# Queue places for the weight sums of an MLP's second map: behind the neighbouring product's split and weight load

## The chip, the cores and the metric

The kernel runs on one core of one Trainium2 chip. Its time is the device time of one execution in microseconds (us); the time of a kernel is the median of three runs. Five engines with a queue each take part: PE (TensorE, matmuls), DVE (VectorE, additions and subtractions), ACT (ScalarE, copies and activations), POOL (GpSimd, here only for issuing DMAs that store) and SP (SyncE, only for issuing DMAs, nearly all loads). An engine takes the instructions of its queue in order, so one that waits holds up all behind it; only PE's weight loads run beside its matmuls.

## The reference

One layer of a decoder, S = 2048 tokens, D = 1024, hidden width 4096, fp32:

```python
h = x * (1.0 + sc1) + sh1
z = h @ w_in[l]                                   # token mixing: conv and pooling groups
...
x = _layer_norm(DEEPNORM_ALPHA * x + (1.0 + g1) * mix, ln1_g[l], ln1_b[l])
h = x * (1.0 + sc2) + sh2
f = jnp.square(jax.nn.relu(h @ w_mlp_in[l])) @ w_mlp_out[l]
x = _layer_norm(DEEPNORM_ALPHA * x + (1.0 + g2) * f, ln2_g[l], ln2_b[l])
```

## The kernel before

**Stages.** The tokens are worked on in two halves of 1024 (b = 0 and 1). For each half come the input projection, the output projection with the first norm, and then the **first map** (`first_map(b)`: h times w_mlp_in, ReLU, square). After both halves, one **second map** (`down`) multiplies the squared hidden values of all 2048 tokens by w_mlp_out and ends with the last norm. The text calls the first maps of the two halves map 0 (about 280 to 700 us of the profiled span) and map 1 (about 920 to 1265 us).

**Products.** Every fp32 operand is split in two: `hi`, a copy rounded by ACT (L135), and `lo`, the rest, subtracted by DVE (L136). Three matmuls (L140, L141, L142: hi·hi, hi·lo, lo·hi) stand for one fp32 matmul; the L142 one is the only one that reads the weight's `lo`. Maps are computed by Strassen's method in Winograd's form: seven products of sums of blocks instead of eight products of blocks. In the first map a block of 512 hidden columns (`up(b, g, …)`, g = 0 to 7) takes seven products of 24 matmuls each. For each product `product` (inside `seven`) takes a raw weight tile `r` of 128x1024 (a block of w_mlp_in, or a sum of blocks), splits it into a pair of `w` tiles, and runs the matmuls into two PSUM banks. Tiles of a name share a ring of fixed size: r 5, w 6 (three pairs), o 10, h 28, PSUM 8.

**Where the weights of the first map come from.** In map 0, from g = 2 on, `block_weights` loads four raw blocks (SP, L566), forms the sums on DVE and stores them for map 1 (`w1sum`); in map 1, and for g < 2, `summed_weights` loads each tile as it is (SP, L598).

**Work beside the products in the first map.** Results in PSUM are added by DVE (`add`, `o<-o,ps` rows at L145), made ReLU and square by ACT, and then `sums` forms the quarter sums that the second map's Strassen form wants (DVE, 128x256 rows at L145), each stored by POOL to `usum` (L1058).

**The weight sums of the second map** (`sum_down`, L1124 to L1137). The second map has 26 products, and most of them want a sum of blocks of w_mlp_out (`in_w2`). They are formed in eight groups. A group takes three `o` tiles (L1126) and holds them over its 11 **steps**; in all it has 12 loads of 128x512 (SP, L1136, 256 KB each), 20 additions of 128x512 (DVE, L145) and 17 stores to `wsum` (POOL, L1134, 256 KB each). The first step only loads; each later one adds, stores and reloads half tiles, so that a reload waits for the store of what stood there, and a later addition waits for the reload.

A step is traced where `next` is called on the generator. In map 0, `first_side` first yields a few other pieces, with 16 steps among them, then all the steps that are left, one per call; in map 1 the side is the generator itself; `down` takes one step per position of its stream. In the maps the call is `beside()`, 48 times in each map after the opening products (1 in g = 0, 5 in g = 1, 7 in each later block). The second map's stream has a position for each pair of a product and a quarter of the contraction (`gp`), 24 matmuls each; its operands are four positions ahead: a load of `r<-usum`, a load of `w<-in_w2` or `w<-wsum` (L1173, L1175), a split each into `h` tiles.

**What sets the order.** The order in which code is traced is not the order of an engine's queue. A scheduler places every instruction in its engine's queue by its own reckoning of when its inputs are there, and may set work that is traced later ahead of work that waits. `with tc.issue_after(x)` holds it back in one respect: instructions traced in the block that run on x's engine stand behind x in that engine's queue. It is an order of the queue, not a wait of its own.

Of the kernel before, what the change touches and what calls it, by code (L numbers as in the profile page):

```python
# [97 lines left out]
def tile_hybrid_layer(ctx: ExitStack, tc: tile.TileContext, opening, xT, x, wada, win,  # L98
# [23 lines left out]
    def t_w(dt=F32R):  # L122
        return mk(big, [P, T], dt, "w", 6)
# [10 lines left out]
    def split(src, hi, lo):  # L134
        high = nc.scalar.copy(hi, src)  # L135
        return high.ins, nc.vector.tensor_tensor(lo, src, hi.bitcast(F32), op=ALU.subtract).ins  # L136
# [7 lines left out]
    def tt(out_, a, b_, op):  # L144
        return nc.vector.tensor_tensor(out_, a, b_, op=op)  # L145
# [183 lines left out]
    def parts(src, t=t_h):  # L329
        hi, lo = t(), t()  # L330
        split(src, hi, lo)
        return hi, lo
# [224 lines left out]

    RAW = range(4)  # L560
    ORDER = (("11", "11"), ("12", "21"), ("s2", "2"), ("s1", "1"), ("s3", "3"), ("s4", "22"), ("22", "4"))

    def block_weights(src, dst=None):
        a11, a12, a21, a22 = [t_r() for _ in range(4)]
        for i, r in enumerate((a11, a12, a21, a22)):
            nc.sync.dma_start(r, src[i])  # L566
        yield a11
        yield a12
        s1 = t_r()
        tt(s1, a21, a22, ALU.add)  # L570
        tt(a21, a11, a21, ALU.subtract)
        tt(a11, s1, a11, ALU.subtract)
        tt(a12, a12, a11, ALU.subtract)
        if dst is not None:
            for i, r in enumerate((s1, a11, a21, a12)):
                nc.gpsimd.dma_start(dst[i], r)
        for r in (a11, s1, a21, a12, a22):
            yield r
# [16 lines left out]
    def summed_weights(src, sums, order):  # L595
        for i in order:
            r = t_r()
            nc.sync.dma_start(r, src[i] if i in RAW else sums[i - 4])  # L598
            yield r

    def seven(ready, B, first_w=None):
        made = [first_w] if first_w else []

        def product(i, banks, new):
            hi, lo = made.pop() if made else parts(next(ready), t_w)
            for p in range(2):
                if new:
                    banks[p] = t_ps()
                for k in range(4):
                    bh, bl = B[ORDER[i][1], k // 2]  # L610
                    ks = slice((k % 2) * H, (k % 2) * H + H)
                    cs = slice(p * H + k * P, p * H + k * P + P)
                    mm3(banks[p], hi[:, cs], lo[:, cs], bh[:, ks], bl[:, ks], new and k == 0, k == 3,
                        not new)

        return product
# [406 lines left out]
    def up(b, g, B, beside, turn):  # L1023
# [11 lines left out]

        def add(r, banks):
            for p in range(2):
                tt(r[:, ps[p]], r[:, ps[p]], banks[p], ALU.add)

        def join(r, banks):  # L1040
            add(r, banks)
# [112 lines left out]
    def down(g2, close, side):  # L1154
# [92 lines left out]
        for k, (n, gp) in enumerate(stream):  # L1247
            if n == last:
                break
            next(side, None)  # L1250
            if k + 4 < len(stream):
                ready.append(operand(*stream[k + 4]))
            ops = ready.pop(0)
            _, _, _, new, reads = PRODUCTS[n]
            if gp == 0:
                if new:
                    banks[n % 2] = [t_ps() for _ in range(4)]
                if 3 <= n < 12:
                    next(later)
            for i in range(4):  # L1260
                unit(banks[n % 2][i], i, ops, new and gp == 0, gp == 3, not new)
            if gp == 3:
                for t, d, c in reads:
                    read(t, d, c, banks[n % 2])
                    if final[t, d] == n:
                        finish(t, d)
# [82 lines left out]
    def first_side():  # L1349
        for n in range(0, 8, 2):  # L1350
            ada(G2 + n, G2 + n + 2, nc.sync.dma_start, lambda: t_o(D))
            yield
        for n in range(4):
            for _ in range(4):
                next(sums_down)
                yield
            sum_x(n)
            yield
        g2 = mk(sm, [P, D], F32, "bc", 1)
        row_by_dram(g2, mod[:, G2 : G2 + KD], 1)  # L1360
        gate.append(g2)
        for p in halves:
            sum_weights(wins[0], winsum, t_o, which=[p])
            yield
        for _ in sums_down:
            yield

    gate = []
# [2 lines left out]
    def first_map(b, B, back):  # L1371
        side = sums_down if b else first_side()
        open_ = []

        def beside():
            if open_:
                next(side, None)

        def turn():
            if b + 1 < NB:  # L1380
                ready.append(prepare())

        ups = [up(b, g, B, beside, turn) for g in range(NC)]
        for g in range(2):
            next(ups[g])
            back(1 + g)
        for i in range(3, 7):
            next(ups[0])
            back(i)
        open_.append(True)  # L1390
        for g in range(NC):
            for _ in ups[g]:
                pass
# [62 lines left out]
```

## Time and profile before

| | |
|---|---|
| runs | 1849.01, 1844.09, 1844.26 us; median 1844.26 us |
| profiled execution | 1848.79 us, of which the span of the profile is 1846.8 us |
| PE busy | 1726.5 us (93% of the span), 7519 matmuls |
| DVE busy | 1420.4 us (77%) |
| ACT, POOL busy | 840.1 us (45%), 402.7 us (22%) |
| moved by DMA | 478.95 MB, mean 259 GB/s |
| stores to wsum | 136 of 256 KB, median 4.5 us from issue to landing |
| loads of blocks for the sums (o<-in_w) | 104 of 256 KB, median 5.0 us (8 of them for the input projection's sums) |

All times in the rows below are us from the start of the span. In a row of a group of instructions (`line engine op out<-in`), the last columns are the busy time, the mean duration of one, and the time that the engine stood idle just before them with what ended it. In a row of stretches, `(x178)` is the number of instructions, and the last three columns are the clock that TensorE was granted, the busy share of the DMA engines and the GB/s. A row of waits reads: which line waited for which line, us in total, how many times, longest. In a row of the timeline the first column is the start, the second the time that the merged instructions took together; consecutive instructions start a little before the one ahead has ended, so that two 128x512 additions in a row start 0.60 us apart though each takes 0.69 us.

### The profile page before, as it was taken

The page shows a single profiled execution, that of the slowest core. Times are in us where ns is not written, and L with a number is a line of the kernel's source. Part 1 is how long each engine was busy: PE and PEld are TensorE (multiplying, and loading weights), DVE is VectorE, ACT ScalarE, POOL GpSimd, SP SyncE. Part 2 cuts the span into 40 slices and gives each one's busy share as a digit, 9 for nine tenths or more (in the row PEclk, how much of TensorE's full clock was granted, in tenths as well). Part 3 has the DMA queues.
Part 4 walks back from the last instruction along what each step waited for, and adds up shares of the span by engine and source line. Part 5 has one row for each costly group of instructions (what it writes and reads, how often), then busy time and mean ns, then how long its engine had stood idle before and what let it go on. Part 6 is the DMA issues. An engine that isn't in the chain of part 4 may idle for free. (4 is left out here: it accounts for less than half of the span.)

```text
span 1846.8 us, 22581 instructions
## 1 busy us (share of the span) xinstructions
PE 1726.5 (93%) x7519; PEld 1415.0 (77%) x7519; DVE 1420.4 (77%) x2222; ACT 840.1 (45%) x1148; POOL 402.7 (22%) x767
## 2 busy tenths in 40 slices
PE   9999998777959889999988999899999999999998
PEld 8888886656747768888866777677888888888887
DVE  7997886687877877689676677777666586686998
ACT  6322475334534465344754344453644334353552
POOL 0223121244454531010113454443000000000000
PEclk9999998888989999999989999999999999999999
DMA  9998864588988896257545798898967787676772
GB/s 389 349 337 316 305 248 158 184 300 296 314 291 289 287 309 232 100 189 260 185 158 173 268 292 288 276 304 307 353 235 260 247 281 282 219 249 219 266 279 80
DMA packets 155205, 478.95 MB, mean 259 GB/s; under 512 B 22600, under 2 KB 23120, under 8 KB 155088
## 3 DMA queue, kind: packets, MB, share of 16 engines
q1 hardware_dynamic: 100960, 304.44, 47.8%
q0 software_dynamic: 54128, 173.07, 26.1%
q8 instruction: 59, 0.97, 0.2%
q14 instruction: 58, 0.48, 0.1%
HBM read 315.40 MB, written 162.01 MB: 259 GB/s over the span
## 5 line engine op out<-in xcount | busy, mean ns | idle before, releaser
L140 PE MATMUL ps<-h,w 128*128 128x512 f32 x1312 | 523.9, 400 | 58.8 <-ACT w L135 34.5
L142 PE MATMUL ps<-h,w 128*128 128x512 f32 x1312 | 522.7, 399 | 38.2 <-DVE w L136 38.2
L141 PE MATMUL ps<-h,w 128*128 128x512 f32 x1312 | 521.9, 398 | 8.1 <-DVE h L136 8.0
L141 PE MATMUL ps<-h,h 128*128 128x512 f32 (+1 forms) x1064 | 414.3, 389 | 3.5 <-DVE h L136 3.5
L140 PE MATMUL ps<-h,h 128*128 128x512 f32 (+1 forms) x1064 | 414.0, 389 | 0.8 <-ACT h L135 0.8
L142 PE MATMUL ps<-h,h 128*128 128x512 f32 (+1 forms) x1064 | 414.1, 389 | 0.0
L140 PEld LDWEIGHTS ps<-h,w 128*128 128x128 f32 x1312 | 252.5, 193 | 118.5 <-ACT w L135 37.3
L142 PEld LDWEIGHTS ps<-h,w 128*128 128x128 f32 x1312 | 253.1, 193 | 97.6 <-DVE w L136 44.6
L145 DVE TENSOR_TENSOR o<-o,o 128x256 f32<-128x256 f32 (+2 forms) x554 | 266.0, 524 | 70.5 <-DMA o<-in_w 23.9
L141 PEld LDWEIGHTS ps<-h,w 128*128 128x128 f32 x1312 | 253.1, 193 | 64.3 <-DVE h L136 11.1
L1058 POOL DMA_DIRECT2D usum<-o x416 | 222.9, 541 | 245.6 <-DVE o L145 172.9
L135 ACT CAST w<-r 128x1024 fp32r<-128x1024 f32 x156 | 163.4, 1050 | 203.5 <-PE ps L141 175.9
L135 ACT CAST h<-r 128x1024 fp32r<-128x1024 f32 (+1 forms) x144 | 144.8, 1011 | 240.4 <-PE ps L141 131.1
L141 PEld LDWEIGHTS ps<-h,h 128*128 128x128 f32 x1064 | 200.6, 189 | 45.3 <-DVE h L136 4.3
L136 DVE TENSOR_TENSOR h<-r,h 128x1024 fp32r<-128x1024 f32 (+1 forms) x144 | 167.5, 1170 | 86.0 <-ACT h L135 85.8
L140 PEld LDWEIGHTS ps<-h,h 128*128 128x128 f32 x1064 | 200.7, 189 | 42.5 <-ACT h L135 1.6
L142 PEld LDWEIGHTS ps<-h,h 128*128 128x128 f32 x1064 | 200.6, 189 | 40.8
L136 DVE TENSOR_TENSOR w<-r,w 128x1024 fp32r<-128x1024 f32 x156 | 190.0, 1222 | 49.4 <-ACT w L135 48.7
L145 DVE TENSOR_TENSOR o<-o 128x256 f32<-128x256 f32 (+1 forms) x240 | 124.9, 528 | 69.2 <-DMA o<-in_w 38.6
L145 DVE TENSOR_TENSOR o<-o,ps 128x512 f32<-128x512 f32 x172 | 114.1, 683 | 22.9 <-PE ps L142 19.5
L136 DVE TENSOR_TENSOR h<-w,h 128x1024 fp32r<-128x1024 f32 x104 | 126.8, 1220 | 1.6 <-ACT h L135 1.5
L1134 POOL DMA_DIRECT2D wsum<-o x136 | 73.5, 541 | 191.3 <-DVE o L145 185.1
(163 smaller groups left out, 1382.4 us busy)
## 6 DMA issues: line engine op xcount, KB each, us to landing
usum<-o POOLq DMA_DIRECT2D x416, 128.0 KB, 4.9
r<-usum SPq DMA_DIRECT2D x104, 512.0 KB, 5.1
wsum<-o POOLq DMA_DIRECT2D x136, 256.0 KB, 4.5
w<-wsum SPq DMA_DIRECT2D x68, 512.0 KB, 5.6
r<-in_w SPq DMA_DIRECT2D x54, 512.0 KB, 5.3
o<-in_w SPq DMA_DIRECT2D x104, 256.0 KB, 5.0
r<-w1sum SPq DMA_DIRECT2D x40, 512.0 KB, 4.8
w<-in_w SPq DMA_DIRECT2D x36, 512.0 KB, 6.3
```

The lines of the kernel that those rows point to most:

```text
L135: high = nc.scalar.copy(hi, src)
L136: return high.ins, nc.vector.tensor_tensor(lo, src, hi.bitcast(F32), op=ALU.subtract).ins
L140: nc.tensor.matmul(ps, whi, xhi, start=first, stop=False, skip_group_check=goes_on)
L141: nc.tensor.matmul(ps, whi, xlo, start=False, stop=False, skip_group_check=goes_on)
L142: nc.tensor.matmul(ps, wlo, xhi, start=False, stop=last, skip_group_check=goes_on)
L145: return nc.vector.tensor_tensor(out_, a, b_, op=op)
L1058: nc.gpsimd.dma_start(usum[slot, g // 2, :, b, g % 2, :], z)
L1134: nc.gpsimd.dma_start(wsum[i - 8, g // 2][:, cs], regs[to])
```

## The change

Four things change.

1. Two **marks** are kept while the program is traced: the last load of a first-map weight on SP, and the last `lo` half of a weight split or the last half of a PSUM addition on DVE, whichever was traced later.
2. In both maps `beside()` traces its step inside two `issue_after` blocks, one for each mark: the step's DVE work stands behind the DVE mark, its SP loads behind the SP mark. ACT and POOL get no mark.
3. `first_side` ends with 17 steps (3 · 11 − 16) instead of all that are left, so that map 0 forms exactly three groups (33 steps); its last 5 calls find nothing. Before, map 0 traced 38 steps: three groups and 5 steps of the fourth.
4. `down` takes two steps per position instead of one. Map 1 takes 48 steps in both kernels; before, that leaves 2 of the 88 for `down`, now 7.

```diff
@@ block_weights, summed_weights
+    mark = {}
...
-            nc.sync.dma_start(r, src[i])
+            mark["SP"] = nc.sync.dma_start(r, src[i]).ins
...
-            nc.sync.dma_start(r, src[i] if i in RAW else sums[i - 4])
+            mark["SP"] = nc.sync.dma_start(r, src[i] if i in RAW else sums[i - 4]).ins
@@ seven
-            hi, lo = made.pop() if made else parts(next(ready), t_w)
+            if made:
+                hi, lo = made.pop()
+            else:
+                r = next(ready)
+                hi, lo = t_w(), t_w()
+                mark["DVE"] = split(r, hi, lo)[1]
@@ up
-                tt(r[:, ps[p]], r[:, ps[p]], banks[p], ALU.add)
+                mark["DVE"] = tt(r[:, ps[p]], r[:, ps[p]], banks[p], ALU.add).ins
@@ down
-            next(side, None)
+            for _ in range(2):
+                next(side, None)
@@ first_side
-        for _ in sums_down:
+        for _ in range(3 * len(W_SUMS) - 16):
+            next(sums_down)
             yield
@@ first_map
-                next(side, None)
+                with tc.issue_after(mark["DVE"]), tc.issue_after(mark["SP"]):
+                    next(side, None)
```

Every engine has as many instructions as before; only their order in the queues differs. Three places show it. Names carry a running number for the tile (`o_692`), so the same tile may have other numbers in the two programs; line numbers behind the diff's first lines grow by 1 to 9 (L1136 becomes L1142, L598 becomes L599, L664 becomes L670).

**First place: SP's queue at the end of map 0**, where the loads of the second half's input projection begin (`in_xT`, `xsum`: the tokens and their sums; `in_wins`, `winsum`: its weights). `o_692` to `o_694` are the three tiles of the fourth group of weight sums. Before:

```order
L598 DMA r_703_5176<-in_wins 128x1024
L664 DMA r_706_5182<-in_xT 128x2x512
L1136 DMA o_692_5080<-in_w2 128x512 x2
L1136 DMA o_693_5081<-in_w2 128x512
L664 DMA r_709_5191<-in_xT 128x2x512
L1136 DMA o_694_5082<-in_w2 128x512
L1136 DMA o_692_5080<-in_w2 128x512
L664 DMA r_712_5200<-in_xT 128x2x512
L664 DMA r_715_5209<-in_xT 128x2x512
L1136 DMA o_694_5082<-in_w2 128x512
```

With the change:

```order
L599 DMA r_700_5159<-in_wins 128x1024
L670 DMA r_703_5165<-in_xT 128x2x512
L670 DMA r_706_5174<-in_xT 128x2x512
L670 DMA r_709_5183<-in_xT 128x2x512
L670 DMA r_712_5192<-in_xT 128x2x512
L670 DMA r_715_5201<-xsum_147 128x2x512
L670 DMA r_718_5207<-xsum_147 128x2x512
L670 DMA r_730_5348<-xsum_147 128x2x512
```

The fourth group's loads are gone from here, and with them its additions on DVE; before, the scheduler had set all 11 steps of it ahead, those that are traced only in map 1 too. In the changed kernel they stand in map 1.

**Second place: DVE's queue in map 1** between the splits of two weight tiles that follow each other (`w_1129`, `w_1133`, block g = 1; 1005 to 1008 us of the profile before). The `o_1107` to `o_1109` rows of 128x512 with no `ps` are additions of the fourth group; the 128x256 rows are quarter sums. Before:

```order
L145 TENSOR_TENSOR o_1109_7646<-o_1109_7646,o_1032_7206 128x256
L136 TENSOR_TENSOR w_1129_7865<-r_1127_7862,w_1128_7864 128x1024
L145 TENSOR_TENSOR o_1109_7646<-o_1109_7646,o_1032_7206 128x256
L145 TENSOR_TENSOR o_1113_7701<-o_1113_7701,ps_1117_7715 128x512
L136 TENSOR_TENSOR w_1133_7920<-r_1131_7917,w_1132_7919 128x1024
```

With the change the second split has 17 instructions between it and the first (one row stands for two); the last eleven and the split:

```order
L145 TENSOR_TENSOR o_1106_7621<-o_1029_7181,o_1106_7621 128x256
L145 TENSOR_TENSOR o_1106_7621<-o_1106_7621 128x256
L145 TENSOR_TENSOR o_1080_7445<-o_1080_7445,o_1106_7621 128x256
L145 TENSOR_TENSOR o_1106_7621<-o_1106_7621 128x256
L145 TENSOR_TENSOR o_1107_7642<-o_1107_7642,o_1109_7644 128x512
L145 TENSOR_TENSOR o_1106_7621<-o_1106_7621,o_1029_7181 128x256
L145 TENSOR_TENSOR o_1108_7643<-o_1107_7642,o_1108_7643 128x512
L145 TENSOR_TENSOR o_1106_7621<-o_1106_7621,o_1029_7181 128x256
L145 TENSOR_TENSOR o_1119_7718<-o_1119_7718,ps_1051_7286 128x512
L145 TENSOR_TENSOR o_1119_7718<-o_1119_7718,ps_1052_7299 128x512
L145 TENSOR_TENSOR o_1108_7643<-o_1108_7643,o_1107_7642 128x512
L136 TENSOR_TENSOR w_1133_7897<-r_1131_7894,w_1132_7896 128x1024
```

The first split has moved ahead of the quarter sums, and steps of the fourth group stand ahead of the second.

**Third place: SP's queue at the start of the second map.** The `r<-usum` and `w<-in_w2` loads of 128x1024 are its operands; `o_1301` to `o_1303` before and `o_1327` to `o_1329` now are the eighth group's tiles. Before:

```order
L1173 DMA r_1353_9952<-usum_140 128x1024
L1136 DMA o_1303_9512<-in_w2 128x512
L1136 DMA o_1302_9511<-in_w2 128x512
L1136 DMA o_1303_9512<-in_w2 128x512
L1136 DMA o_1301_9510<-in_w2 128x512
L1175 DMA w_1342_9930<-in_w2 128x1024
L1175 DMA w_1348_9942<-in_w2 128x1024
L1136 DMA o_1302_9511<-in_w2 128x512
L1175 DMA w_1354_9954<-in_w2 128x1024
```

With the change:

```order
L1179 DMA r_1353_9930<-usum_140 128x1024
L1142 DMA o_1327_9730<-in_w2 128x512 x2
L1142 DMA o_1328_9731<-in_w2 128x512
L1181 DMA w_1342_9908<-in_w2 128x1024
L1142 DMA o_1327_9730<-in_w2 128x512
L1181 DMA w_1348_9920<-in_w2 128x1024
L1142 DMA o_1329_9732<-in_w2 128x512
L1181 DMA w_1354_9932<-in_w2 128x1024
L1181 DMA w_1360_9944<-in_w2 128x1024
L1142 DMA o_1329_9732<-in_w2 128x512
```

Before, the loads above are the last of the eighth group. Now they are its first, and six more follow further down, between the operand loads of the positions that come later (the last of them stands behind the operands of position 11). On DVE the group's additions stand accordingly between the splits of the second map's operands.

## The prediction

> **What bounds the kernel now.** I read the page's busy shares first, then PE's row in 40 slices, then the stretches of 40 us, then what PE waits for in the two first maps.
>
> ```profile
> PE 1726.5 (93%) x7519; PEld 1415.0 (77%) x7519; DVE 1420.4 (77%) x2222; ACT 840.1 (45%) x1148; POOL 402.7 (22%) x767
> PE   9999998777959889999988999899999999999998
> ```
>
> PE is the bound, and the slices below 9 lie where the first maps run (a slice is 46 us; counted from 0, slices 6 to 14 are 277 to 692 us, and 20, 21 and 25 lie between 923 and 1200). What can be won is PE's lost time there. The stretches give it:
>
> ```profile
> 400.00:440.00 40.00, 40.00 (x178) 33.13 (x178) 31.58 (x51) 21.51 (x25) 15.33 (x29) 1.00 0.90 314
> 640.00:680.00 40.00, 34.66 (x141) 27.59 (x140) 30.01 (x51) 28.62 (x37) 13.39 (x25) 0.91 0.90 301
> 680.00:720.00 40.00, 34.85 (x141) 27.66 (x140) 31.35 (x42) 21.88 (x28) 8.65 (x17) 0.91 0.92 312
> 1000.00:1040.00 40.00, 40.00 (x178) 33.12 (x178) 29.79 (x61) 20.61 (x25) 19.76 (x37) 1.00 0.76 240
> 1040.00:1080.00 40.00, 36.20 (x152) 29.13 (x151) 32.46 (x61) 16.69 (x20) 19.06 (x37) 0.96 0.87 270
> 1080.00:1120.00 40.00, 36.97 (x163) 30.31 (x162) 27.50 (x53) 18.47 (x22) 18.48 (x35) 1.00 0.85 295
> 1160.00:1200.00 40.00, 33.92 (x141) 26.93 (x140) 30.01 (x58) 13.89 (x18) 18.26 (x35) 0.96 0.84 281
> 1200.00:1240.00 40.00, 38.21 (x169) 31.34 (x168) 30.33 (x58) 18.85 (x23) 20.15 (x38) 1.00 0.92 301
> 1240.00:1280.00 40.00, 37.16 (x149) 29.47 (x148) 30.98 (x58) 17.80 (x21) 16.67 (x31) 0.91 0.87 310
> 1280.00:1320.00 40.00, 38.47 (x169) 31.35 (x168) 26.18 (x24) 27.38 (x34) 3.22 (x6) 1.00 1.01 375
> ```
>
> A stretch without loss holds 178 matmuls, 0.225 us each, so a product of 24 takes 5.4 us. One with 141 has lost 37 · 0.225 = 8.3 us, of which 5.3 us is idle and the rest is matmuls issued slowly after an idle piece, at a granted clock of 0.91. By the same sum 1040, 1080, 1160 and 1200 lost 5.8, 3.4, 8.3 and 2.0 us, together **19.5 us**; 1240 and 1280 lost 6.5 and 2.0. What PE waits for, first from 280 to 720, then from 960 to 1260:
>
> ```profile
> PE ps L140 <- ACT w L135: 34.5, 6, 18.6
> PE ps L142 <- DVE w L136: 25.5, 9, 10.0
> ```
>
> ```profile
> PE ps L142 <- DVE w L136: 12.7, 5, 3.6
> ```
>
> So in map 1 the late thing is the weight's `lo` half, a subtraction on DVE. DVE is busy only three quarters of the time: the split is late because of what stands ahead of it. In map 1 this is, by shape:
>
> ```profile
> L145 DVE TENSOR_TENSOR o<-o,o 128x256 f32<-128x256 f32 x120 | 44.1, 420 | 1.2 <-ACT o L1046 1.1
> L145 DVE TENSOR_TENSOR o<-o,o 128x512 f32<-128x512 f32 x42 | 28.9, 689 | 13.1 <-DMA o<-in_w 12.6 <-DMA usum<-o 0.3
> L145 DVE TENSOR_TENSOR o<-o 128x512 f32<-128x512 f32 x30 | 20.5, 690 | 29.8 <-DMA o<-in_w 23.5 <-DMA usum<-o 3.6 <-issue 2.7
> ```
>
> The 128x256 rows are quarter sums; the two 128x512 rows hold the weight sums, at whose head DVE stands 36 us for their loads.
>
> **The change, term by term**, against the profiled execution (1848.8 us, of which 1846.8 is span), whose stage lengths I take. The instruction counts don't change, so nothing is saved or paid but waiting. SP's loads and POOL's stores move with each step.
>
> **Term D, map 1's dense places (gain).** A group before is done in about seven products, now over nine to eleven, as the order has it. The worst place before:
>
> ```profile
> 1092.81 1.23 DVE L136 TENSOR_TENSOR w<-r,w 128x1024 fp32r<-128x1024 f32 x1
> ...
> 1107.36 0.69 DVE L145 TENSOR_TENSOR o<-o 128x512 f32<-128x512 f32 x1 [2.34 <-DMA o<-in_w]
> ...
> 1110.44 1.22 DVE L136 TENSOR_TENSOR w<-r,w 128x1024 fp32r<-128x1024 f32 x1
> ```
>
> ```profile
> 1111.72 0.50 PE L142 MATMUL ps<-h,w 128*128 128x512 f32 x1 [3.03 <-DVE w L136]
> ```
>
> Two splits lie 17.6 us apart; two products of PE take 10.8. Between them stand 23 quarter sums (0.335 us start to start, as the two rows at 621 below show), 7 weight sums and an addition from PSUM (0.60 each), and waits for loads of 3.9 us. In the changed queue the matching pair has the same 23 and 5, the PSUM additions being elsewhere, and I put the wait at 2.4: 7.7 + 3.0 + 2.4 = 13.1 us. That still exceeds 10.8, by 2.3 where it was 6.8. Splits are made ahead into three pairs, so some of that is covered, but the start of a group still falls on the longest run of quarter sums. I take half of the 19.5 us: **+9.8**, with bounds of 0 (gaps only change place) and 19.5 (all gone).
>
> **Term C, the fourth group's start now in map 1 (loss).** The stretch from 1000 had all 178 matmuls and gets the first half of the fourth group: between the splits of w_1129 and w_1133 stand 17 instructions instead of 2, about 7.5 us instead of 0.9, and reloads to wait for. The three stretches of before with a group's start (1080, 1160, 1200) lost 3.4, 8.3 and 2.0, on average **−4.6**, which I take; bounds 0 and −8.3.
>
> **Term B, the end of map 0 (gain).** There the fourth group goes away. From 640 to 700 PE waits:
>
> ```profile
> PE ps L142 <- DVE w L136: 5.9, 4, 2.1
> PE ps L140 <- ACT w L135: 4.6, 2, 2.5
> ```
>
> That is 10.5 us, of which one wait of 1.3 lies ahead of the fourth group, beside the third:
>
> ```profile
> 641.53 0.50 PE L142 MATMUL ps<-h,w 128*128 128x512 f32 x1 [1.27 <-DVE w L136]
> ```
>
> For the others SP and DVE show the cause: SP's queue, what it waits for between 655 and 700, and DVE:
>
> ```profile
> 681.98 0.35 SPq L1136 DMA_DIRECT2D o<-in_w  x1
> 682.43 0.38 SPq L598 DMA_DIRECT2D r<-winsum  x1
> ```
>
> ```profile
> SPq L1136 <- DMA wsum<-o: 10.7, 3, 6.8
> ```
>
> ```profile
> 690.06 1.22 DVE L136 TENSOR_TENSOR h<-r,h 128x1024 fp32r<-128x1024 f32 x1 [1.12 <-ACT h L135]
> ```
>
> The load of the next product's weight stands behind a reload of the fourth group that waited for a store; the splits come late from there. With the group gone, the waits of 9.2 us (10.5 less 1.3) and their slow restarts can go, about 5 of the 6.1 us (two stretches of 8.3, less 10.5 idle). The loads of the input projection's tokens and sums still have to come, 512 KB each. I take **+11** of 14.2; bounds 0 and 14.2.
>
> The skill bears on the slow restarts. The Trainium skill, in "TensorE: Matmul & The Clock Gate", Part 1, says that the array falls to half clock after an idle window of about 3.4 us, of a counter that runs free. By this, the waits here (the longest 2.5 us) would cost only themselves, and terms B and D would be about 8 and 8. The trace only half agrees: 640 to 680 has no wait over 2.5 us and was granted 0.91, while 1080 to 1120 with one of 3.03 us was granted 1.00.
>
> **Term A, the middle of map 0 (both signs).** The marks act in map 0 too. The wait for DVE that takes longest there, and another:
>
> ```profile
> 450.99 0.69 DVE L145 TENSOR_TENSOR o<-o,o 128x512 f32<-128x512 f32 x1 [4.07 <-ACT o L642]
> 451.60 1.22 DVE L136 TENSOR_TENSOR w<-r,w 128x1024 fp32r<-128x1024 f32 x1
> ```
>
> ```profile
> 621.46 0.42 DVE L145 TENSOR_TENSOR o<-o 128x256 f32<-128x256 f32 x1
> 621.79 0.42 DVE L145 TENSOR_TENSOR o<-o,o 128x256 f32<-128x256 f32 x1
> ...
> 624.40 1.22 DVE L136 TENSOR_TENSOR w<-r,w 128x1024 fp32r<-128x1024 f32 x1
> ```
>
> ```profile
> 625.68 0.64 PE L142 MATMUL ps<-h,w 128*128 128x512 f32 x1 [2.64 <-DVE w L136]
> ```
>
> At 451 the split that PE waited 10.0 us for stood right behind the addition that waited for ACT. Now six instructions stand between: a 128x1024 subtraction (1.14 us) and five of 128x512 (0.60 each), 4.1 us later. At 534 two weight sums now precede the subtraction that PE's 18.6 us wait hangs on: −1.5. At 638, four weight sums more ahead of a split: −2.4. At 624 the split now stands ahead of the seven quarter sums and two PSUM additions that held it: the wait of 2.6 us can go, with its restart, +4 (my estimate, 1.4 for the restart). Sum **−4**; bounds −9 (nothing regained at 624, restarts elsewhere) and +4.
>
> **Term E, the start of the second map.** The eighth group moves behind the map's end: 12 loads and 17 stores of 256 KB, 7.6 MB, into a stretch whose DMA engines are full (1280 to 1320: share 1.01, 375 GB/s). What carries its prices:
>
> ```profile
> SPq L1136 <- DMA wsum<-o: 93.9, 26, 7.3
> ```
>
> ```profile
> wsum<-o POOLq DMA_DIRECT2D x136, 256.0 KB, 4.5
> o<-in_w SPq DMA_DIRECT2D x104, 256.0 KB, 5.0
> ```
>
> ```profile
> 1259.14 0.86 SPq L1175 DMA_DIRECT2D w<-in_w  x2
> ```
>
> ```profile
> 1268.23 0.80 PE L141 MATMUL ps<-h,h 128*128 128x512 f32 x1 [2.57 <-DVE h L136]
> ```
>
> SP stood 26 times for such stores between 960 and 1300, 3.6 us each. A round trip is addition 0.6, store issue 0.5, store 4.5, load 5.0: 10.6 us, and by the order four of them follow one another until the splits of position 8 can pass: 42 us from about 1262 (my estimate: SP's 1259 and part of a load), so 1304. PE, starting the second map at 1268, wants position 8 at 1268 + 8 · 5.4 = 1311. So 7 us are in hand, and this costs nothing but contention. In return the first operand's weight load, which was issued at 1259 behind reloads of the eighth group, can go earlier (part of the 6.5 us lost in 1240 to 1280), though five weight sums now stand ahead of its split. I take **−1**; bounds −20 (below) and +3.
>
> Sum: 9.8 − 4.6 + 11 − 4 − 1 = **+11 us**: 1837.6 against the profiled execution. That one lies 4.5 us over the median of the three runs, so on the median 1844.3 − 11 = **1833 us**.
>
> **The rivals.**
> 1. *All places clear.* The even spread gives every split its time: D 19.5, C 0, B 14, A −2, E 0: 31 us, 1813. For it: DVE is at 77%, and a cycle of seven products has 38 us. Against: the queue order still puts the group's start in the run of 23 quarter sums.
> 2. *The gaps move.* D 0 and C −4.6 because each group now meets a longer stretch of products, B 8, A −4, E −1: −2 in all, 1846, within the noise. For it: map 1's five waits are of 2.5 us on average, and one late load of a group makes such a wait anywhere.
> 3. *Slower: the eighth group's round trips in the full DMA queue.* If a round trip takes over 12.5 us instead of 10.6 (50 us for four, 1262 + 50 = 1312), the additions on DVE hold the splits, and the reloads on SP hold the operand loads behind them, each for the other. With half again as long legs (15.9 us) position 8 comes 14 us late and the fifth round trip 5 more: E −20, and with B and D at two thirds (7, 6.5): 1844.3 + 15 = 1859; at the forecast's B and D, 1852. For it: 1.01 and 375 GB/s before anything is added. Against: the 169 matmuls of 1280 to 1320 show that operands came nearly in time though the engines were full. The Trainium skill, in "DMA: Bandwidth & Descriptors", Latency and other measured facts, gives 0.2 us for an access to memory on average and 2 us at high load; by this a round trip of two transfers could grow by 3.6 us to 14.2, past the point. No row shows a store in that stretch.
> 4. *Only idle time comes back*, by the clock rule above: B 8, D 8, the rest as it was: 6 us, 1838.
> 5. *The change doesn't do what it says*: ACT has no mark, and a late copy there (34.5 us of waits in map 0) holds the splits as before. The order shows the moves, so this is small, and it gives rival 2's time.
>
> **How the numbers follow.** Chances: forecast 0.40, rival 1 0.15, rivals 2 and 5 0.20, rival 3 0.20, rival 4 0.05. About 0.3% (5.5 us) is what a measurement of this kernel can tell from no change: faster means below 1838.7, slower above 1849.8. Rival 4 lies on the edge and is shared out. Faster 0.40 + 0.15 + 0.02 = 0.57; same 0.23; slower 0.20. The terms' bounds, taken together as independent, give about ±15 around 1833; the range reaches to rival 3's middle, 1855, and stops at 1815, near rival 1: what is left out is half of each.
>
> **What would show it.** Right: no `o<-in_w` load between 655 and 720 and 178 matmuls, or nearly, in 680 to 720; PE's waits for `DVE w L136` in map 1 at about half of 12.7 us, with a new one near 1010; the wait at 442 longer by 4 us and that at 623 gone. Wrong: PE waiting for `DVE h L136` after 1290, with SP's L1142 rows behind `wsum<-o`, means rival 3; map 1's stretches again at 141 to 163 matmuls mean rival 2.

## The result and the profile after

The changed kernel takes 1848.03 us in the median of ten runs (1843.29 to 1851.13), the kernel before 1846.19 us in ten runs beside it: ratio **1.0004, 95% interval 0.9988 to 1.002**. Nothing that can be measured. The forecast was 1833, 11 us less; of the rivals, the second (the gaps move, 2 us) comes nearest.

The page's first lines and PE's row of the kernel after:

```profile
span 1845.5 us, 22577 instructions
## 1 busy us (share of the span) xinstructions
PE 1723.2 (93%) x7519; PEld 1414.0 (77%) x7519; DVE 1416.8 (77%) x2222; ACT 842.6 (46%) x1148; POOL 402.4 (22%) x767
...
PE   9999998777969789999988999998999999999998
```

Each engine has the busy share that it had, within 1%. The stretches of the kernel after (busy times by engine, granted clock, DMA share, GB/s), beside those of before in the prediction and the one of before that it lacks, which comes first here:

```profile
1120.00:1160.00 40.00, 39.49 (x174) 32.39 (x173) 31.35 (x60) 18.47 (x23) 20.14 (x39) 1.00 0.88 277
```

```profile
640.00:680.00 40.00, 34.43 (x139) 27.62 (x140) 26.71 (x40) 29.02 (x37) 9.33 (x19) 0.87 0.72 238
680.00:720.00 40.00, 35.64 (x148) 28.22 (x147) 30.08 (x43) 22.52 (x30) 6.76 (x13) 0.96 0.72 235
1000.00:1040.00 40.00, 38.81 (x163) 31.68 (x164) 32.71 (x69) 19.40 (x25) 22.57 (x43) 0.96 0.84 272
1080.00:1120.00 40.00, 40.00 (x178) 33.14 (x177) 30.81 (x59) 19.42 (x23) 20.76 (x39) 1.00 0.90 295
1120.00:1160.00 40.00, 35.30 (x144) 28.67 (x144) 26.31 (x52) 16.63 (x19) 16.79 (x32) 0.92 0.85 274
1160.00:1200.00 40.00, 40.00 (x177) 33.05 (x176) 30.36 (x59) 16.25 (x19) 19.85 (x38) 0.99 0.93 306
1200.00:1240.00 40.00, 37.05 (x164) 30.36 (x163) 31.71 (x62) 19.70 (x23) 20.32 (x38) 1.00 0.85 276
1240.00:1280.00 40.00, 33.77 (x141) 27.18 (x140) 29.84 (x55) 17.14 (x20) 18.72 (x35) 0.91 0.97 336
1280.00:1320.00 40.00, 40.00 (x178) 33.06 (x177) 28.96 (x32) 26.79 (x33) 6.00 (x12) 1.00 0.97 368
```

The worst stretches of before, 1080 (163 matmuls) and 1160 (141), are whole now; 1120, which had 174, has 144, 1000 has 163 instead of 178, and 1200 164 instead of 169. What PE waits for, first from 280 to 720, then from 960 to 1260:

```profile
PE ps L140 <- ACT w L135: 39.1, 5, 18.1
PE ps L142 <- DVE w L136: 22.9, 8, 5.2
```

```profile
PE ps L142 <- DVE w L136: 11.3, 4, 4.7
```

Four waits of 11.3 us in place of five of 12.7. Matmuls stand in the same order of products in both programs, so the start of the n-th matmul after, less its start before, says how far the one lags, and the difference over a stage says what was lost (+) or won (−) there. All kernels below are read in this way against the trace of before (us; single executions, on different chips):

| stage, by before's times | predicted | after | no marks | marks in map 1 | four tiles, marks in map 1 | no reloads, no stores | no additions |
|---|---|---|---|---|---|---|---|
| 319 to 648, middle of map 0 (A) | +4 | +8.6 | +3.8 | +2.0 | −1.5 | +6.1 | +7.9 |
| 648 to 702, end of map 0 (B) | −11 | −8.7 | −8.7 | −7.3 | −4.4 | −9.1 | −9.0 |
| 996 to 1032, fourth group's start (C) | +4.6 | +5.6 | +5.5 | +5.9 | +7.7 | +8.4 | +2.7 |
| 1032 to 1241, dense places (D) | −9.8 | −5.4 | +5.2 | −6.0 | −14.1 | −20.9 | −20.9 |
| from 1241, second map (E) | +1 | −0.3 | +7.2 | +0.1 | −0.3 | −5.0 | +1.7 |

A column can be off by a few us: the kernel before is one execution here, and its median was 1853.0 us on the chip of the two columns without and with marks in map 1, 1846 to 1848 on the others.

What holds PE is seen best at the longest wait in map 1, first DVE, then SP, POOL and PE:

```profile
1138.80 2.10 DVE L145 TENSOR_TENSOR o<-o,o 128x256 f32<-128x256 f32 x6
...
1146.71 0.43 DVE L145 TENSOR_TENSOR o<-o 128x256 f32<-128x256 f32 x1
1151.21 0.69 DVE L145 TENSOR_TENSOR o<-o 128x512 f32<-128x512 f32 x1 [4.07 <-DMA o<-in_w]
1151.82 1.35 DVE L145 TENSOR_TENSOR o<-o,o 128x256 f32<-128x256 f32 x3
1153.09 1.22 DVE L136 TENSOR_TENSOR w<-r,w 128x1024 fp32r<-128x1024 f32 x1
```

```profile
1146.76 9.13 SPq L1142 DMA_DIRECT2D o<-in_w  x2
```

```profile
1140.92 0.54 POOL L1140 DMA_DIRECT2D wsum<-o  x1 [2.94 <-DVE o L145]
```

```profile
1154.36 0.79 PE L142 MATMUL ps<-h,w 128*128 128x512 f32 x1 [4.70 <-DVE w L136]
```

A store issued at 1140.92, a reload that had to wait until that store had landed and went out at 1146.76, and the addition that reads it at 1151.21, 10.3 us after the store: DVE stands 4.1 us with the split behind it. Over map 1 and the start of the second map (960 to 1300) DVE's waits for these loads are, before and after:

```profile
DVE o L145 <- DMA o<-in_w: 36.5, 22, 4.5
```

```profile
DVE o L145 <- DMA o<-in_w: 45.3, 15, 7.3
SPq L1142 <- DMA wsum<-o: 146.4, 33, 10.9
```

The first row of the second fence is DVE's, the other SP's. Fewer waits, but longer, and more in all. The same holds for the dense places alone (1032 to 1241, before and after):

```profile
DVE o L145 <- DMA o<-in_w: 30.0, 19, 4.5
```

```profile
DVE o L145 <- DMA o<-in_w: 35.1, 10, 7.3
```

Not each of them holds PE. The two longest, 7.3 and 7.1 us at 1088 and 1126, held no matmul: the splits around them lie 9.7 and 9.9 us apart, less than the two products that take 10.8. The one of 4.1 us above stands in a run of 23 quarter sums, and its splits lie 15.4 us apart.

### The profile page after: what moved, and what is told of

It reads as the page before. It is cut to its first block, busy times and chain, and to the rows that moved or that the text cites. A ratio compares the mean times of both kernels' runs of the same rounds, so it can differ in the third digit from the quotient of the medians.

```text
span 1845.5 us, 22577 instructions
## 1 busy us (share of the span) xinstructions
PE 1723.2 (93%) x7519; PEld 1414.0 (77%) x7519; DVE 1416.8 (77%) x2222; ACT 842.6 (46%) x1148; POOL 402.4 (22%) x767
## 4 chain that ended last, share of the span: by engine, by line
PE 48%; DMA 10%; DVE 9%; issue 5%; POOL 2%; ACT 1%; SPq 0%; DVEq 0%; POOLq 0%; ACTq 0%
PE ps L142 16%; PE ps L141 16%; PE ps L140 16%; DVE o L145 6%; DMA o<-in_w 3%; DMA wsum<-o 3%; DMA usum<-o 2%; DVE w L136 2%; POOL usum L1064 1%; DMA r<-in_w 1%; DMA r<-winsum 1%; DVE h L136 0%; DMA o<-hsave 0%; DMA o<-in_xT 0%; POOL wsum L1140 0%
## 5 line engine op out<-in xcount | busy, mean ns | idle before, releaser
L135 ACT CAST h<-w 128x1024 fp32r<-128x1024 f32 x104 | 108.8, 1046 | 18.2 <-DVE w L145 9.7
```

## The experiments

All times are ratios to the kernel before, run on the same chip between the runs of the other kernels. I had two theories to begin with: that each place has a price of its own, so that parts of the change add up; and that the loss is set by the number of weight sums and only changes place. Later ones asked what the price at a place consists of.

**Which part does what.** Without the mark of SP every engine's queue is word for word that of the change. So the effect of the marks is that of the DVE mark. The three kernels keep the 17 steps and the two steps per position and differ in the marks:

```diff
 no marks:
-                with tc.issue_after(mark["DVE"]), tc.issue_after(mark["SP"]):
-                    next(side, None)
+                next(side, None)
 marks in map 1 only (in map 0 only: b == 1):
+                if b == 0:
+                    next(side, None)
+                    return
```

No marks: 

> The change without its marks: 17 steps at the end of the first side and two steps per position of the second map stay; beside the products each step is placed as before. The fourth group leaves the end of map 0 and starts in map 1; the rest of map 0 is queued as before the change. Theory (each place has its own price, the places' prices add up): the trace of the changed kernel, matmul by matmul against before, gained 8.4 us at the end of map 0 and lost 5.6 us where the fourth group starts (998 to 1034 us); the other places are those of before, so about 3 us faster than before, no marked waits moved in map 0, and map 1 keeps its dense places. Rival (the loss is set by how many weight sums DVE has beside the maps, and only changes place): within 2 us of before. Rival that the marks cost nothing and the count alone spoils it: 5 us or more slower than before.

Measured: **1.0043 (1.0025 to 1.0061)**, 8 us slower; by the number that is the last rival, but the next run takes away its reason, that the marks cost and bring nothing.

Marks in map 1 only: 

> The change with its marks in map 1 only; map 0 is queued as before up to the third group and without the fourth. Theory (places add up): what the changed kernel lost from 456 to 656 us, 8.5 us, goes, its gains at the end of map 0 (8.4) and in map 1's dense places (5.4) and its loss at the fourth group's start (5.6) stay: about 8 us faster than before, near 1838 beside 1846. Rival (the loss only changes place): within 2 us of before, as the change itself.

Measured: **0.9975 (0.9962 to 0.9989)**, 4.6 us faster, where 8 were expected.

Marks in map 0 only: 

> The change with its marks in map 0 only; map 1 takes its steps unmarked, in dense groups as before. Theory (places add up): the loss of 8.5 us in the middle of map 0 stays, the end of map 0 gains 8.4, the fourth group's start costs 5.6, the dense places cost as before: about 6 us slower than before. Rival (the loss only changes place): within 2 us of before.

Measured: **1.008 (1.0059 to 1.0101)**, 15 us slower, where 6 were expected; most of what is more lies from 1241 on (9.4 us lost in its trace).

With the change itself this is a square. Marks in map 0 cost 5 to 7 us (0.9975 to 1.0004; 1.0043 to 1.008), marks in map 1 bring 12.5 to 14 us (1.0043 to 0.9975; 1.008 to 1.0004), nearly the same beside each other: the parts add up, and the second theory is out. But the count alone costs 8 us where I had expected a gain of 3: without the marks the shift of the fourth group into map 1 wins 8.7 us at the end of map 0, and then loses 5.5 at its start, 5.2 at the dense places and 7.2 at the second map (its trace loses 13 us in all, the runs 8). In that kernel PE's longest wait in map 1 is this one:

```profile
1073.10 0.80 PE L142 MATMUL ps<-h,w 128*128 128x512 f32 x1 [7.94 <-DVE w L136]
```

So marks and count only together come to nothing: +8 − 13 + 5.

**Steps away from the long runs of quarter sums**, the place where the prediction saw the trouble. On the kernel with marks in map 1, `beside` takes a number of steps, in map 1 the seven calls of a block take 1, 2, 2, 2, 0, 0, 0:

```diff
-        def beside():
-            if open_:
+        def beside(n=1):
+            if b == 0:
+                n = 1
+            for _ in range(n if open_ else 0):
...
```

> As the kernel with marks in map 1 only, and in map 1 no step is taken around the two longest runs of quarter sums of a block (the last three of its seven calls); the first of the seven takes one step and the next three two each. 8 groups are made as before. Theory (a split is late where weight sums fall into the run of 23 quarter sums that a split has to wait for): the waits that the changed kernel has at 1069, 1150 and 1206 us (2.5, 4.7 and 2.9 us, with slow matmuls behind some of them) go, about 8 to 12 us less than the kernel with marks in map 1 only. Rival (the waits are set by the round trips of the reloads, wherever the additions stand): the waits move to the products in which two steps now follow each other, and the time is within 3 us of the kernel with marks in map 1 only.

Measured: **1.0042 (1.0023 to 1.0061)**, 12 us slower than the kernel with marks in map 1, so neither. The waits for splits did go, as the theory says (from 11.8 to 0.5 us between 960 and 1300), and the waits moved, as the rival says, but at a price that neither had. PE, then DVE, from 960 to 1300:

```profile
PE ps L140 <- DVE o L145: 20.2, 6, 6.8
```

```profile
DVE o L145 <- DMA o<-in_w: 42.6, 22, 5.4
DVE o L145 <- DMA wsum<-o: 11.6, 3, 5.6
DVE o L145 <- DMA usum<-o: 11.1, 2, 7.9
```

Now the opening matmuls of products wait for additions from PSUM (`o<-o,ps`), and these stand behind weight sums that wait: the longest, 6.8 us at 1092, behind three waits of 5.6, 2.0 and 3.7 us on DVE. The waits for reloads are hardly more than with marks in map 1 (40.7 us there); those for stores are. By the trace 12 of the 15 us that it loses against that kernel lie from 1241 on; why there was not asked further.

**What a place costs: DVE's work, or its wait?** First all reloads of map 1 and the second map were left out (eight of the 12 loads of a group; the expectation says nine), and the stores made to read a tile that nothing overwrites:

```diff
-                        nc.gpsimd.dma_start(wsum[i - 8, g // 2][:, cs], regs[to])
-                for to, i in loads:
+                        nc.gpsimd.dma_start(wsum[i - 8, g // 2][:, cs], regs[to] if g < 3 else gate[0][:, :H])
+                for to, i in loads if g < 3 or (5, 7) in loads or not adds else ():
```

> The changed kernel, but from the fourth group on (map 1 and the second map) nine of the 12 loads of a group, the reloads, are left out and its stores read a fixed tile, so that no addition of a weight sum waits for a reload or a store; all additions stand where they stood on DVE. The second map then gets other numbers in those weight sums, at the same cost. Theory (waits): in the changed kernel DVE stands 45 us for o<-in_w between 960 and 1300, in the middle of queues that hold a split, and this makes PE's waits of 2.5, 4.7, 2.9 and 5.8 us at 1069, 1150, 1206 and 1271 with the slow matmuls behind them: 14 to 20 us faster than the changed kernel, so about 0.990 of before. Rival (work): the splits are late because 23 quarter sums and four or five weight sums, 11 us of DVE work, stand between two of them; then at most 5 us faster, 0.997 or more.

Measured: **0.9997 (0.9984 to 1.001)**; by that, no gain. But the trace lost 17.0 us in stage A and 1.5 in B where the changed kernel wins 8.7, and from 1032 on won 28.6. The stores waited for nothing any more, POOL has no mark, and they had moved into map 0 and the stage behind it (560 to 741 us):

```profile
680.00:720.00 40.00, 30.62 (x113) 22.41 (x112) 27.18 (x49) 24.21 (x31) 23.42 (x44) 0.91 1.03 376
```

POOL has 44 issues there instead of 13, and the DMA engines are full. The run alone decides nothing. Then without these stores (the second map reads the first two groups' sums in their place):

```diff
-                    if i >= 0:
+                    if i >= 0 and g < 3:
...
-            nc.sync.dma_start(q, w2[w, gp] if w < 8 else wsum[w - 8, gp])
+            nc.sync.dma_start(q, w2[w, gp] if w < 8 else wsum[w - 8, 0])
```

> The kernel without reloads again, now with the stores of the fourth to eighth group left out as well (the second map reads the first two groups' sums in their place, as many bytes). In the run without reloads the stores, which then waited for nothing, had moved to the end of map 0, where DMA was at 1.03 and 21 us were lost, while from 1027 us on 20 us were gained. Theory (waits for reloads hold the splits): with map 0 as in the changed kernel the whole gain shows, 15 to 22 us against the changed kernel, 0.988 to 0.993 of before. Rival (work on DVE): the additions stand where they stood, so at most 5 us, 0.997 or more.

Measured: **0.9892 (0.9871 to 0.9914)**, 20 us faster. All 20 additions of a group stand on DVE nearly where they stood; PE's waits from 960 to 1300:

```profile
PE ps L140 <- ACT h L135: 3.4, 1, 3.4
PE ps L141 <- DVE h L136: 3.0, 3, 1.1
PE ps L140 <- ACT o L1039: 1.7, 1, 1.7
PE ps L142 <- DVE w L136: 1.4, 1, 1.4
```

11.3 us for splits fell to 1.4. The opposite, 18 of the 20 additions left out and every load and store kept:

```diff
+                    if g < 3 or i in (8, 9):
-                    tt(regs[to], regs[x], regs[y], ALU.add if sign > 0 else ALU.subtract)
+                        tt(regs[to], regs[x], regs[y], ALU.add if sign > 0 else ALU.subtract)
```

> The changed kernel, but from the fourth group on 18 of the 20 additions of a group are left out; all its loads and stores stay, so that SP still stands for stores and the DMA engines move the same bytes. The second map gets other numbers in those weight sums, at the same cost. Both theories of DVE (waits or work at the weight sums) expect the same gain or a little more than without the reloads, 14 to 22 us against the changed kernel, 0.990 of before or less. Rival (SP and the DMA engines): the loads of the first map's weights and of the second map's operands stand behind loads of the weight sums that wait for stores, and that makes splits late by their own data; then the waits stay, within 5 us of the changed kernel.

Measured: **0.9897 (0.9884 to 0.991)**, 19 us faster. The traffic is all there: SP still stood 122 us for stores to wsum between 960 and 1300 (146 in the changed kernel). In the dense places the two runs win the same 20.9 us, one with all additions and the other with all traffic, so there neither the additions' own 0.6 us nor the traffic cost anything that the table shows: the price of a place is the **wait of an addition** that stands ahead of a split. That the two totals agree is in part chance. Where the fourth group starts, additions that wait for no reload still cost something (8.4 us lost, 2.7 without them), and from 1241 on the kernel that keeps the traffic loses 6.7 us more than the one without it. Neither was taken apart.

**Taking the waits away with the sums kept.** First four groups back in map 0, so that map 1 has only four, spread by the marks, and the second map none:

```diff
-        for _ in range(3 * len(W_SUMS) - 16):
-            next(sums_down)
-            yield
+        for i in range(4 * len(W_SUMS) - 16):
+            next(sums_down)
+            if i < 16 or i % 2:
+                yield
```

> Marks in map 1 only; map 0 forms four groups as before the change (the last 12 steps two at a call), map 1 the other four with the marks, and the second map none. Theory (places add up): against the kernel with marks in map 1 only (0.9975 of before) the end of map 0 loses the 5 to 8 us that it had gained, the start of a group at 1000 us still costs about 5, one group less in map 1 gains about 5 and the second map's first wait of 5.8 us and its restart go: within 3 us of that kernel. Rival (the number of weight sums beside the maps sets the loss): slower by 5 us or more, since map 0 gets a group more and map 1 only a step less.

Measured: **1.0027 (1.0012 to 1.0043)**. Against the kernel with marks in map 1 it loses 18 us at the end of map 0 (+10.8 instead of −7.3) and wins 8.6 at the second map. The rival's 5 us or more have come, but at the end of map 0 and not in map 1, which wins 3 us in the dense places. At the end of map 0 two steps stand at a call, and PE's waits from 640 to 730 there are

```profile
PE ps L142 <- DVE w L136: 20.0, 4, 9.7
```

Whether the additions' work, their waits (9.0 us on DVE for reloads and stores there) or late loads hold these splits is not shown; the two runs above left map 0 as it was.

Then another table of the steps, with the same additions, loads and stores in the same three tiles, but each reload issued a step earlier (the first rows of it):

```diff
-    ((), ((0, 4), (1, 6), (3, 2))),
-    (((2, 0, 1, -1, 8), (4, 3, 1, -1, 9)), ((5, 7),)),
-    (((1, 1, 5, -1, 10), (3, 1, 3, -1, 11)), ((4, 1), (0, 0))),
+    ((), ((0, 4), (1, 6), (2, 2), (3, 7))),
+    (((0, 0, 1, -1, 8), (4, 2, 1, -1, 9)), ((5, 1), (4, 0))),
+    (((1, 1, 3, -1, 10), (2, 1, 2, -1, 11)), ()),
```

In the changed kernel: 

> The changed kernel with another table of the 11 steps: the same 20 additions, 12 loads and 17 stores of a group, in the same three tiles, but each reload is issued one step before the step that it used to stand in, so that two products instead of one lie between a reload and the addition that reads it. Theory (a round trip of 10.6 us is longer than the 5.4 us between two steps): the waits for o<-in_w in map 1 fall from 45 us to under 20, PE's waits at 1069, 1150 and 1206 us shrink or go, and the time is 6 to 15 us below the changed kernel, 0.992 to 0.997 of before. Rival (work, or the stores that a reload must wait for in so few tiles): within 3 us of the changed kernel.

With marks in map 1 only: 

> The same table of steps in the kernel with marks in map 1 only (0.9975 of before). Theory: the gains add up, 0.990 to 0.995 of before. Rival: as without the table, 0.9975.

Measured: **1.0024 (1.001 to 1.0038)** and **1.0026 (1.0011 to 1.0041)**: no gain in either. The first is about what the rival says; the second is 9 us slower than without the table, which neither had. By the traces 7.4 of these 9 us are lost in the middle of map 0, where the table holds too (+9.4 instead of +2.0). DVE's and SP's waits of the first of the two, 960 to 1300:

```profile
DVE o L145 <- DMA o<-in_w: 41.9, 15, 8.6
```

```profile
SPq L1142 <- DMA wsum<-o: 138.4, 26, 12.9
```

A reload that stands earlier in SP's queue only waits longer there (5.3 us each instead of 4.4): in three tiles the half tile that it goes to is mostly one whose store has been issued in the same step. So the same table with a fourth tile (eight half tiles, a reload takes the one that has been free for longest):

```diff
-            tiles = [t_o() for _ in range(3)]
+            tiles = [t_o() for _ in range(4)]
```

> As the run before it, with four tiles for a group instead of three, so that a reload takes a half tile that has been free for longest. Theory of the waits: where reloads still wait for a store, this takes that away too, 2 to 6 us below the kernel with three tiles. Rival: the ring of ten tiles then has one less for the first map's results, and their copies wait; slower than with three by 3 us or more.

Measured: **0.9942 (0.9923 to 0.9961)**, 11 us faster than before and the fastest kernel here that computes everything. DVE, then PE from 960 to 1300:

```profile
DVE o L145 <- DMA wsum<-o: 29.3, 12, 4.8
DVE o L145 <- DMA o<-in_w: 5.8, 4, 2.0
```

```profile
PE ps L142 <- DVE w L136: 6.6, 5, 2.2
PE ps L141 <- DVE h L136: 6.6, 4, 4.1
```

Waits for reloads fell to 5.8 us, from 38.0 in the kernel with the same table and marks in three tiles (45.3 in the changed kernel); a part of them came back as additions that wait to overwrite a half tile whose store is still under way (29.3 us, from 13.4). Against that kernel the trace wins 10.9 us in the middle of map 0 and 10.2 in the dense places, and loses 4.3 at the end of map 0. Last, the same tiles and table in the kernel before:

> The kernel before (no marks, all remaining steps in the first side, one step per position) with the table of steps and the four tiles of the run on four tiles (0.9942 with the marks in map 1). It tells whether the marks still matter once a reload seldom has to wait. Theory (the waits are what costs, the place only decides which split they hit): most of the gain comes without the marks, 0.990 to 0.996 of before. Rival (marks and tiles each bring their own part, the marks 12 us as in the kernels with three tiles): 0.998 to 1.002.

Measured: **0.999 (0.9978 to 1.0002)**, the rival's 0.998 to 1.002. The trace wins 6.8 us at the dense places and loses 4.2 at the end of map 0, where the fourth group still stands. So the tiles do not bring the gain alone. Which they need, the marks in map 1 or the shift of the fourth group, was not run apart.

## Why the prediction was wrong

The direction of terms A to D was right and E was about nothing, but the sum of +11 us shrank to about +1 in the trace, nothing in the runs. A and D each fell 4.5 us short, B 2.3 and C 1.0. Term by term, by the table above:

- **The step that failed is the wait for reloads, in term D**: "In the changed queue the matching pair has the same 23 and 5 … and I put the wait at 2.4", down from 3.9, from which it takes half of all that the dense places lost. At the matching pair (1097.94 to 1109.80) the working came out better than that: 23 quarter sums, 5 weight sums, no wait at all, 11.9 us, and no matmul held. But the waits for reloads did not fall with it. In the dense places they went from 30.0 us in 19 to 35.1 us in 10, and one of 4.1 us stood in another run of 23 quarter sums, at 1151, where PE then waited 4.7 us. So D brought 5.4 us, not 9.8. I took it that steps spread more thinly would meet fewer reloads under way. They met fewer and longer ones: by the rows above a store and its reload took 10.3 us, and the next step follows a product of 5.4 us later. The marks set where these waits stand and not how long they are in all: without marks they were 46.0 us between 960 and 1300, with marks in map 1 only 40.7. With the waits gone and the additions kept, the dense places win 20.9 us, so the price was in the part that I had guessed.
- **Term A** had the same fault. It counted four additions at 638, 2.4 us. There the changed kernel's split stands behind a wait as well (DVE, then PE):

```profile
644.89 0.69 DVE L145 TENSOR_TENSOR o<-o,o 128x512 f32<-128x512 f32 x1 [2.75 <-DMA o<-in_w]
645.50 1.22 DVE L136 TENSOR_TENSOR w<-r,w 128x1024 fp32r<-128x1024 f32 x1
```

```profile
646.77 0.80 PE L142 MATMUL ps<-h,w 128*128 128x512 f32 x1 [5.24 <-DVE w L136]
```

  Another wait for a reload, 4.5 us on DVE at 600, holds a split that PE then waits 1.8 us for at 603; with the slow matmuls behind it 3.7 us went there, for which the sum has no term. 8.6 us were lost instead of 4; the kernels with unmarked map 0 lost 2 to 4 in that stage with before's order, so 5 to 7 belong to the marks, as the square of runs says. No run takes these waits alone away, so this cause is read from the rows and not tested. At 442 the wait moved from 10.0 to 7.6 and 3.0 us, so the 4 us that I had put there are nearly absent; at 624 the wait went, as predicted.
- **Term B** was right in kind, 8.7 us instead of 11: waits of 1.7 and 2.5 us were left at 682 and 690.
- **Term C** has the size, 5.6 instead of 4.6, by luck. The two splits between which it counts 17 instructions (at 999.10 and 1008.70, 9.6 us apart) held no matmul, and a later one cost a wait of 1.1 us at 1031. About 4 of the 5.6 us are lost before that, around this wait:

```profile
1000.09 0.80 PE L140 MATMUL ps<-h,w 128*128 128x512 f32 x1 [1.68 <-ACT o L1039]
```

  It is for a copy out of PSUM by ACT, which has no mark and now makes a weight's `hi` ahead of that copy. The term is also incomplete: the group that starts there delays all behind it. Without marks the later stages lose 12 us.
- **Term E** came out as forecast, about nothing. The first operand's wait fell from 2.57 us at 1266 to 0.47 at 1264 and came back at the second position, whose split stood behind an addition of the eighth group that waited for its load (DVE, then PE):

```profile
1271.85 0.69 DVE L145 TENSOR_TENSOR o<-o 128x512 f32<-128x512 f32 x1 [1.87 <-DMA o<-in_w]
...
1273.80 1.22 DVE L136 TENSOR_TENSOR h<-r,h 128x1024 fp32r<-128x1024 f32 x1
```

```profile
1276.55 0.79 PE L141 MATMUL ps<-h,h 128*128 128x512 f32 x1 [5.76 <-DVE h L136]
```

- **Rival 3** did not come: the stretch from 1280 ran 178 matmuls at a DMA share of 0.97 with the eighth group's traffic in it, and no operand was late behind it. **Rival 2** has the total, in part by luck: its D of 0 was 5.4 us too low and its A of −4 missed as much the other way. Its reason holds, one late load of a group makes a wait anywhere. It was given 0.20 together with rival 5 and deserved more, since the new length of a wait for a reload could be read from no row. ACT, at which rival 5 points, is where most of C was lost.

What stays open: why stage A loses 2 to 4 us in runs whose map 0 is queued as before up to 643 us; the executions were taken on different chips, and the table is no finer than that.

## What to carry to other kernels

When work with loads in it is moved in an in-order queue, price the wait of each moved instruction for its own data before its duration: here, in the dense places, the additions of four to five groups cost nothing that could be seen once they did not wait, and 15 us with their waits (−20.9 against −5.4). Placing a step exactly behind its neighbour only helps once its data are there by then, and that is a question of buffers (a fourth tile took DVE's waits for reloads from 38 to 6 us), not of issuing a load earlier in a queue that waits for the same store. A change that bundles several moves should be taken apart: this one held a gain of 13 us, a loss of 8 and a loss of 5.

## What was not expected of the hardware

Half speed after an idle piece does not go by the length of the piece alone. Two stretches of the kernel before, each in two rows: the first has a wait of 2.04 us that ends at 1068.68, the second one of 3.03 us that ends at 1111.72.

```profile
1066.21:1069.62 3.41, 1.36 (x6) 0.81 (x6) 3.41 (x9) 0.83 (x1) 2.26 (x5) 1.00 1.10 297
1069.62:1073.04 3.42, 3.42 (x10) 2.63 (x9) 3.42 (x8) 0.00 (x0) 2.38 (x5) 0.50 0.99 268
1107.16:1110.57 3.41, 1.53 (x7) 0.94 (x5) 3.21 (x7) 1.05 (x1) 3.41 (x7) 1.00 0.92 334
1110.57:1113.99 3.42, 2.27 (x10) 1.88 (x11) 3.42 (x5) 1.06 (x1) 1.67 (x4) 1.00 0.68 240
```

The shorter wait was followed by 3.4 us at a granted clock of 0.50, the longer by none. In every trace here all changes of the granted clock lie on a grid of 3.41 us, and the rows are cut on it. The shorter wait fell whole into one piece of the grid, 2.05 us without PE (3.41 less 1.36); the longer was divided over two, 1.88 and 1.15 us. From 280 to 1310 us of all 14 traces full clock was halved behind no piece of the grid with less than 1.7 us without PE, and behind every one with more than 1.95. The Trainium skill, in "TensorE: Matmul & The Clock Gate", Part 1, describes an activity window of about 3.4 us that runs free, and half clock after an idle one; the grid agrees with this, but a window need not be idle throughout, as a little over half was enough here. So a wait of 2 us can cost a restart, and rival 4, where only idle time comes back, does not hold.
